# Loading a hybrid encoder's two short row groups as half rows over all partitions, casting the first block by channel halves, and splitting the last scaling

## The chip, the cores and the metric

One core of a Trainium2 chip. The metric is the device time in microseconds (us); lower is better. Three runs of the kernel before gave 919.87, 920.51 and 922.76 us, so its median is 920.51 us. The profile is of one more execution, which took 922.18 us.

## The reference, cut to what matters

One layer of an encoder over 2048 prompt frames and 32 sample frames of 1024 channels, all in float32:

```python
hn   = rmsnorm(h, g_mix)                       # h * rsqrt(mean(h*h) + 1e-6) * g_mix
proj = hn @ w_in                               # 1024 -> 3072: hA, bA, cA, zA, vB, zB, 512 each
yA   = bA * conv3(cA * hA) * silu(zA)          # short causal convolution
yB   = (pool(vB) @ pool_w) * pool_scale * silu(zB)
h    = h + concat(yA, yB) @ w_out
gate = sigmoid(rmsnorm(h, g_ple) @ w_ple_gate)
h    = h + (p @ w_ple) * gate
y    = rmsnorm(h, g_final)
```

It returns y for prompt and sample, and the last rows of the two mixers' inputs as states. The change touches the first line for the first frames, and the last line for the last frames.

## The kernel before, in words

The 2080 frames go through three stages on one core: the input projection with both mixers (frames as columns), the output projection, and the gate with the final norm (frames as rows). A float32 product is made of three TensorE products of "hi" and "lo" parts: hi is the operand rounded to the format fp32r, lo is the operand minus hi, and hi·hi, hi·lo and lo·hi are added in PSUM.

**Blocks.** In the first stage the frames are cut in five blocks of 416 (NB, line 25). A block is three tiles of 128 rows and one short group of 32 rows. The rows must be normalized while they are rows (one rstd for each) and then turned, so that channels lie on the partitions: eight TensorE transposes for a tile of 128 rows, four for each half of the channels.

**The start** (lines 382 to 724), on which most of the change bears. SyncE (SP) issues the loads in this order: the norm's weights gm_row (L383); the x rows of block 0's tiles 0, 1 and 2, of 512 KB each, and then the short group, as rows 384 to 415 of block 0 and of block 1 on 64 partitions, one load of 128 KB for each block (all L412, called at lines 630 and 631); the weights of the first three products, raw_firstzb, raw_firstv and raw_firstc, 512 KB each in rows of 512 bytes (L529); six small loads into rows (L772 to L777); raw_pw (L790); and then the three tiles of block 1 (L412 again). For each tile:

- ScalarE (ACT) squares the rows and sums them (L93); GpSimd (POOL) makes the mean (L72) and the power -1/2 (L76);
- VectorE (DVE) multiplies by rstd and by the norm's weights, which lie in two PSUM banks pg[0] and pg[1], one half of the channels each (L641, two instructions a tile);
- TensorE transposes (L433 for tiles, L650 for the short group) into a PSUM bank for each half;
- first_hi (L663) casts a turned half to fp32r, on ACT but for the last one, which is on DVE; first_lo (L667) subtracts, on DVE.

fill (L393) sends TensorE transposes of the identity that nobody reads: seven before the first tile, and two, three and two behind tiles 0, 1 and 2 (line 673). The hi parts of the first weights are cast on ACT (L694, L712), their lo parts on DVE (L703, L716). first_products (L601) then makes three products side by side, zb, v and c, in passes: all hi·hi first, then weight hi by frame lo, then weight lo by frame hi, 8 matmuls of 416 columns for each product and pass (L621). Between them block 1 is prepared step by step (second_block, L728); its short group is the other half of the short tile.

**Order.** A scheduler orders each engine's instructions when the program is built. in_turn (L633) takes an instruction out of its hands: it goes behind all that the program has issued on that engine up to there. In before the first zb matmul alone is not held (L623). PSUM has six banks in one pool (bank) and two in another (tbank); a bank is given to a new tile when the last reader of the old one is done.

**The end** (last_pair, L1587). The last two row tiles are scaled by their rstd in normed (L1633): DVE does 640 of the 1024 columns (L1637), which SP stores (L1638), ACT does 384 (L1639), which are stored through the queue of POOL for the first of the two tiles and of ACT for the last one (L1640).

Of the kernel before, what the change touches and what calls it, by code (L numbers as in the profile page):

```python
# [9 lines left out]
F32 = mybir.dt.float32  # L10
# [24 lines left out]
def trunk(ctx, tc, x_p, x_s, c_conv, c_pool, p_p, p_s, g_mix, w_in, conv_w, conv_b, pool_w,  # L35
# [308 lines left out]
    with ExitStack() as s1:  # L344
# [53 lines left out]

        hn = {}
# [201 lines left out]
        def first_products(ws):  # L601
# [6 lines left out]
            for a, b in ((0, 0), (0, 1), (1, 0)):  # L608
                if b:
                    next(second)  # L610
                    next(second)
                for kind, w in ws.items():
# [7 lines left out]
                    for k in range(KC):  # L620
                        ins = nc.tensor.matmul(out[kind][:, :NB], w[k // KH][:, k % KH, a], x[k // KH][:, k % KH, b],  # L621
                                               start=a + b + k == 0, stop=a == 1 and k == KC - 1, skip_group_check=True)
                        if a + b + k or kind != "zb":  # L623
                            in_turn(ins)
# [5 lines left out]
        ahead0 = [x_load(f"0_{c}", [x_rows(0, c)]) for c in range(3)]  # L630
        short0 = x_load("0_3", [x_rows(0, 3), x_rows(1, 3)])
# [4 lines left out]
        def first_normal(x):  # L636

            xt, m, r = x
            for half in range(2):
# [3 lines left out]
        def first_turn(c, x):  # L643

            xt, m, _ = x
            if c < 3:
                return [turn(x, half, f"pt0_{c}_{half}", bank) for half in range(2)]
            t = short_bank
            for k in range(KC):
                tc.keep_in_program_order(nc.tensor.transpose(t[:, k * m:k * m + m], xt[:m, k * P:(k + 1) * P], ident[:m, :m]))  # L650
            t = t.rearrange("p (k t) -> p k t", k=KC)
            return t[:, :KH], t[:, KH:]
# [3 lines left out]
        def place0(c, half):  # L656
            n = P if c < 3 else DEC
            piece = B0[("11", "21")[half]][:, :, :, c * P:c * P + n]
            return piece[:, :, 0], piece[:, :, 1], turned_x[c][half][:, :, :n]
# [9 lines left out]
        def first_tile(c):  # L669
            first_normal(first_x[c])  # L670
            turned_x[c] = first_turn(c, first_x[c])
            if c < 3:
                fill((2, 3, 2)[c], short_bank)


        for c in range(3):
            first_x.append(x_stat(ahead0[c], True))
        first_tile(0)
        first_hi(0, 0)
        first_x.append(x_stat(short0, True))  # L680
        short0 = first_x[3]
        first_tile(1)
        first_hi(0, 1)
        first_lo(0, 0)
        for half in range(2):
            first_hi(1, half)
        first_tile(2)
        first_hi(2, 0)
        first_tile(3)
        first_hi(2, 1, nc.vector.tensor_copy)  # L690
        raw = raw_weight("zb", 0, "firstzb")
        first_zb = [wtile(f"w_firstzb_{half}") for half in range(2)]
        for half, t in enumerate(first_zb):
            in_turn(nc.scalar.copy(t[:, :, 0], raw[:, half * KH:half * KH + KH]))  # L694
        for half in range(2):
# [1102 lines left out]
```

## Time and profile before

| what | before |
|---|---|
| median of three runs | 920.51 us (919.87 to 922.76) |
| the profiled execution, whole | 922.18 us |
| its span in the trace | 920.4 us |
| TensorE matmuls (PE), busy in the span | 907.0 us, 99% |
| VectorE (DVE), busy | 723.2 us, 79% |
| ScalarE (ACT), busy | 482.7 us, 52% |
| GpSimd (POOL), busy | 159.3 us, 17% |
| granted TensorE clock | 0.998 |

How to read the profile: times in the trace are us from the start of the span. A row of the timeline gives the start, the time from there to the end of the last one of the group, the engine, the source line, the operation, what it writes and reads with the shapes, how many of them there are, and in brackets how long the engine was idle before it and what released it. PE is TensorE's matmul, PEld its weight load; a transpose appears as a weight load of the rows and a matmul with the identity. SPq, ACTq and POOLq rows are DMA issues. L12 is line 12 of the kernel.

### The profile page before, as it was taken

What the parts mean: (1) busy time and instruction counts of PE and PEld (TensorE: products, weight loads), DVE (VectorE), ACT (ScalarE), POOL (GpSimd) and SP (SyncE); (2) the same over time, 40 slices, a digit from 0 to 9 for tenths busy, and PEclk for the clock granted to TensorE, in tenths of its full rate; (3) what the DMA queues carried; (4) which work ended last, traced back from release to release, by engine and by line L of the source; (5) the groups of instructions that cost most, each with busy time, mean ns of one, the idle gap of its engine ahead of it and who ended that gap; (6) DMA issues with size and microseconds to landing.
All of it is one profiled execution on the core that took longest, in us unless ns stands there. A gap on an engine that the chain in (4) does not pass through costs nothing.

```text
span 920.4 us, 13201 instructions
## 1 busy us (share of the span) xinstructions
PE 907.0 (99%) x4529; PEld 824.7 (90%) x4529; DVE 723.2 (79%) x1236; ACT 482.7 (52%) x894; POOL 159.3 (17%) x307
## 2 busy tenths in 40 slices
PE   8999999999999999999999999999999999999996
PEld 6999999999999999999999988888878878888885
DVE  6996898999576989795777579666558658889885
ACT  6744565654345555453444365444436855555554
POOL 2111222121000342310000111111113301111113
PEclk9999999999999999999999999999999999999999
DMA  8357687898945789738885468865767974576554
GB/s 247 100 141 220 170 245 230 244 282 285 416 137 172 235 231 221 231 115 303 245 243 178 146 234 278 266 218 183 237 228 230 357 262 140 206 242 231 190 201 176
DMA packets 138447, 205.12 MB, mean 223 GB/s; under 512 B 13116, under 2 KB 101724, under 8 KB 137101
## 3 DMA queue, kind: packets, MB, share of 16 engines
q1 hardware_dynamic: 117773, 139.41, 47.9%
q0 software_dynamic: 17872, 59.45, 19.6%
q10 hardware_dynamic: 2736, 5.44, 1.6%
q8 instruction: 35, 0.57, 0.3%
q14 instruction: 31, 0.25, 0.1%
HBM read 136.60 MB, written 67.64 MB: 222 GB/s over the span
## 4 chain that ended last, share of the span: by engine, by line
PE 78%; DVE 6%; DMA 3%; issue 1%; ACT 1%; POOL 0%; POOLq 0%; DVEq 0%
PE x_o L175 9%; PE x_g L175 9%; PE x_zab L593 5%; PE z_g L175 5%; PE x_zbv L593 5%; PE e L107 4%; PE z_o L175 4%; PE x_ch L593 4%; PE z_zab L593 3%; PE z_zbv L593 2%; PE z_ch L593 2%; PE y_g L175 2%; PE y_o L175 2%; PE za L593 2%; PE b L593 2%; PE h L593 1%
## 5 line engine op out<-in xcount | busy, mean ns | idle before, releaser
L80 ACT CAST y_S<-y_fS 128x512 fp32r<-128x512 f32 x32 | 19.5, 622 | 36.8 <-PE x_o L175 19.0
L175 PE MATMUL x_g<-wg_b,g_S 128*128 128x512 f32 x128 | 35.7, 390 | 0.0
L175 PE MATMUL x_o<-wo_b,y_S 128*128 128x512 f32 x128 | 35.7, 391 | 0.0
L593 PE MATMUL x_zab<-B,w_zab_S 128*128 128x416 f32 x168 | 34.2, 352 | 0.2 <-ACT V L989 0.2
L593 PE MATMUL z_zab<-B,w_zab_S 128*128 128x416 f32 x168 | 34.3, 352 | 0.0
L593 PE MATMUL x_zbv<-B,w_zbv_S 128*128 128x416 f32 x168 | 34.2, 352 | 0.0
L593 PE MATMUL z_ch<-B,w_ch_S 128*128 128x416 f32 x168 | 34.1, 352 | 0.0
L593 PE MATMUL x_ch<-B,w_ch_S 128*128 128x416 f32 x168 | 34.0, 351 | 0.0
L593 PE MATMUL z_zbv<-B,w_zbv_S 128*128 128x416 f32 x168 | 34.0, 351 | 0.0
L107 PE MATMUL e<-wq,pps 128*128 128x512 f32 x144 | 33.1, 390 | 0.0
L593 PEld LDWEIGHTS x_zab<-B,w_zab_S 128*128 128x128 f32 x168 | 31.3, 188 | 0.8 <-ACT V L989 0.5
L107 PEld LDWEIGHTS e<-wq,pps 128*128 128x128 f32 x144 | 27.0, 188 | 5.6
L593 PEld LDWEIGHTS x_ch<-B,w_ch_S 128*128 128x128 f32 x168 | 31.4, 188 | 0.3
L593 PEld LDWEIGHTS z_zbv<-B,w_zbv_S 128*128 128x128 f32 x168 | 31.4, 188 | 0.3
L593 PEld LDWEIGHTS z_ch<-B,w_ch_S 128*128 128x128 f32 x168 | 31.4, 188 | 0.3
L593 PEld LDWEIGHTS z_zab<-B,w_zab_S 128*128 128x128 f32 x168 | 31.4, 188 | 0.3
L593 PEld LDWEIGHTS x_zbv<-B,w_zbv_S 128*128 128x128 f32 x168 | 31.3, 188 | 0.4
L1343 DVE TENSOR_TENSOR c_o<-x_o,x 128x512 f32<-128x512 f32 x14 | 9.7, 691 | 26.4 <-PE x_o L175 26.4
L1566 DVE SCALAR_TENSOR_TENSOR h<-h,rstd_f,g_bc 128x1024 f32<-128x1024 f32 (+1 forms) x15 | 19.3, 1284 | 14.0 <-POOL rstd_f L76 14.0
L72 POOL TENSOR_SCALAR ms_f<-ssq_f 128x1 f32<-128x1 f32 (+1 forms) x15 | 6.6, 441 | 128.7 <-ACT junk L93 128.5
L175 PEld LDWEIGHTS x_o<-wo_b,y_S 128*128 128x128 f32 x128 | 24.0, 188 | 5.2 <-DVE c_o L1343 0.3
L175 PEld LDWEIGHTS x_g<-wg_b,g_S 128*128 128x128 f32 x128 | 24.0, 188 | 5.0
(591 smaller groups left out, 2688.5 us busy)
## 6 DMA issues: line engine op xcount, KB each, us to landing
y<-y_d SPq DMA_DIRECT2D x16, 512.0 KB, 6.7
x<-in_x_prompt_dram SPq DMA_DIRECT2D x16, 512.0 KB, 4.3
h_d<-x SPq DMA_DIRECT2D x16, 512.0 KB, 3.8
h<-h_d SPq DMA_DIRECT2D x16, 512.0 KB, 3.7
xt<-in_x_prompt_dram SPq DMA_DIRECT2D x15, 512.0 KB, 7.2
e<-e_d SPq DMA_DIRECT2D x15, 512.0 KB, 6.3
out_dram<-h POOLq DMA_DIRECT2D x14, 512.0 KB, 3.0
p_dT<-T POOLq DMA_DIRECT2D x12, 512.0 KB, 6.0
```

The lines of the kernel that those rows point to most:

```text
L72: nc.gpsimd.tensor_scalar(ms[:n], ssq[:n], scalar1=1.0 / D, scalar2=EPS, op0=ALU.mult, op1=ALU.add)
L80: ins = nc.scalar.copy(hi, src)
L107: nc.tensor.matmul(ps, pps[:, a, k], wp[k][b][:, cs], start=k + q == 0, stop=k == 1 and q == 2)
L175: nc.tensor.matmul(ps[:n], lhs[:, k, a, :n], w[b][:, k], start=start and k + q == 0, stop=k == KH - 1 and q == 2, skip_group_check=True)
L593: nc.tensor.matmul(ps[:, :NB], lhs[:, k, x], b[:, k, y], start=start and k + q == 0, stop=stop and k == KH - 1 and q == 2, skip_group_chec ...
L1343: add = lambda o, a, b: nc.vector.tensor_tensor(o, a, b, op=ALU.add)
L1566: nc.vector.scalar_tensor_tensor(h[:n], h[:n], rf[:n], g_bc[:n], op0=ALU.mult, op1=ALU.mult)
```

## The change

The short group now lies as half rows on all 128 partitions: partitions 0 to 63 hold channels 0 to 511 of the 64 short rows, partitions 64 to 127 hold channels 512 to 1023 of the same rows. It is loaded in two loads, one for each half of the channels, both ahead of tile 2. Its sums of squares are therefore half sums, and a matmul with a matrix called pair adds partitions p and p + 64. Its mean is made on DVE out of PSUM. Normalizing takes two instructions of 64 partitions, as before, and the transposes come in two groups of four.

The order of the start is rewritten: the short group's square comes before tile 2's; pg[0] is copied to SBUF early on ACT; tile 2's second half is turned into a bank of the other PSUM pool; the hi casts come by halves of the channels, with the first weights' casts in between; the lo parts come by halves too. The fills behind tiles 0, 1 and 2 are gone; the seven ahead of tile 0 stay. All matmuls of the first products are held in program order, behind the last transposes of the short group, and the transpose of rows (pv) moves behind the first pass.

At the end, for the last tile only, DVE's 640 columns are scaled in two instructions of 320, each with a store of its own on SP.

```diff
+        HP = P // 2
+        pair = one.tile([P, P], F32, name="pair")
+        for h in range(2):
+            nc.vector.tensor_tensor(pair[:, h * HP:h * HP + HP], ident[:, :HP], ident[:, HP:], op=ALU.add)
...
                 if b:
+                    vectors()
                     next(second)
...
-                        if a + b + k or kind != "zb":
-                            in_turn(ins)
+                        in_turn(ins)
...
-        ahead0 = [x_load(f"0_{c}", [x_rows(0, c)]) for c in range(3)]
-        short0 = x_load("0_3", [x_rows(0, 3), x_rows(1, 3)])
+        ahead0 = [x_load(f"0_{c}", [x_rows(0, c)]) for c in range(2)]
+
+        short_x = ring4(xin, "xt_short")
+        for h in range(2):
+            nc.sync.dma_start(short_x[h * HP:h * HP + HP, :NH],
+                              x_p[:2 * NB, h * NH:h * NH + NH].rearrange("(b n) d -> b n d", b=2)[:, 3 * P:])
+        ahead0.append(x_load("0_2", [x_rows(0, 2)]))
...
+            gets = (bank, tbank if c == 2 else bank)
+            return [turn(x, half, f"pt0_{c}_{half}", gets[half], True) for half in range(2)]
+
+        def short_turn(half, t, pin=lambda ins: None):
+
+            hs = slice(half * HP, half * HP + HP)
+            for k in range(KH):
+                pin(nc.tensor.transpose(t[:, k * HP:k * HP + HP], short_x[hs, k * P:k * P + P], ident[hs, hs]))
+            return t.rearrange("p (k b t) -> p k b t", k=KH, b=2)
+
+        def short_sums():
+            ssq = sm.tile([P, 1], F32, tag="ssq", name="ssq_short")
+            in_turn(nc.scalar.activation(junk[:, :NH], short_x[:, :NH], AF.Square, accum_out=ssq))
+            return ssq
+
+        def short_root(ssq):
+            in_turn(nc.tensor.matmul(short_bank[:, :1], pair, ssq, start=True, stop=True))
+            ms, r = (sm.tile([P, 1], F32, tag=t, name=f"{t}_short") for t in ("ms", "rstd"))
+            in_turn(nc.vector.tensor_scalar(ms, short_bank[:, :1], scalar1=1.0 / D, scalar2=EPS, op0=ALU.mult, op1=ALU.add))
+            nc.gpsimd.tensor_tensor(r, ms, nhalf, op=ALU.pow)
+            return r
+
+        def short_half(half, r):
+            hs = slice(half * HP, half * HP + HP)
+            h = short_x[hs, :NH]
+            in_turn(nc.vector.scalar_tensor_tensor(h, h, r[hs], pg[half][hs], op0=ALU.mult, op1=ALU.mult))
+            n = KH * HP
+            turned_x[3, half] = short_turn(half, short_bank[:, half * n:half * n + n], in_turn)[:, :, 0]
...
-            if c < 3:
-                fill((2, 3, 2)[c], short_bank)
...
+        def zb_hi(half, copy=nc.scalar.copy):
+            in_turn(copy(first_zb[half][:, :, 0], raw[:, half * KH:half * KH + KH]))
...
+        for c in range(2):
+            first_x.append(x_stat(ahead0[c], True))
+        short_ssq = short_sums()
+        g_copy = lambda half: nc.scalar.copy(g_bc[:, half * NH:half * NH + NH], pg[half])
+        first_tile(0)
+        in_turn(g_copy(0))
+        first_x.append(x_stat(ahead0[2], True))
+        first_normal(first_x[1], halves=(1, 0))
+        short_r = short_root(short_ssq)
+        turned_x[1] = first_turn(1, first_x[1])
+        first_hi(0, 0)
+        first_hi(1, 0)
+        short_half(0, short_r)
+        first_normal(first_x[2], (0,))
+        first_lo(0, 0)
+        first_normal(first_x[2], (1,))
+        turned_x[2] = first_turn(2, first_x[2])
+        zb_hi(0)
+        first_hi(0, 1)
+        first_hi(3, 0)
+        first_hi(2, 0)
+        short_half(1, short_r)
+        first_hi(1, 1)
+        first_hi(2, 1, nc.vector.tensor_copy)
+        zb_hi(1)
+        first_hi(3, 1)
         for half in range(2):
+            for c in range(4):
                 if c + half:
                     first_lo(c, half)
...
-                fixed(nc.vector.tensor_scalar(o[:, :cut], o[:, :cut], scalar1=rf, scalar2=None, op0=ALU.mult))
-                nc.sync.dma_start(y[:, :cut], o[:, :cut])
+                for cs in (slice(0, cut // 2), slice(cut // 2, cut)) if b else (slice(0, cut),):
+                    fixed(nc.vector.tensor_scalar(o[:, cs], o[:, cs], scalar1=rf, scalar2=None, op0=ALU.mult))
+                    nc.sync.dma_start(y[:, cs], o[:, cs])
```

More of the change, by code (lines that the diff above doesn't have):

```diff
@@ L634, in in_turn, with first_normal @@
             tc.keep_in_program_order(ins)
-        def first_normal(x):
+        def first_normal(x, halves=(0, 1)):
             xt, m, r = x
-            for half in range(2):
+            for half in halves:
                 h = xt[:m, half * NH:half * NH + NH]
@@ L722, in trunk @@
         first_w.extend(other_first(kind) for kind in ("v", "c"))
-        for half in range(2):
-            nc.scalar.copy(g_bc[:, half * NH:half * NH + NH], pg[half])
+        g_copy(1)
         B0["12"] = piece_of(seventh("B0_12"), 0)
@@ L736, in second_block @@
                 yield
[L737 removed]
+            xs.append(((short_x, DEC, None), None))
             whole = []
```

48 lines of the change are left out of this document (12 added, 36 removed).

## The prediction

> **What bounds the kernel now.** First the page: the shares of the engines, then the chain that ended last.
>
> ```profile
> span 920.4 us, 13201 instructions
> PE 907.0 (99%) x4529; PEld 824.7 (90%) x4529; DVE 723.2 (79%) x1236; ACT 482.7 (52%) x894; POOL 159.3 (17%) x307
> PE 78%; DVE 6%; DMA 3%; issue 1%; ACT 1%; POOL 0%; POOLq 0%; DVEq 0%
> ```
>
> TensorE is busy in 907.0 of 920.4 us, and the change leaves its products as they are. So only the 13.4 us without it count, and they lie mostly ahead of the first product and behind the last one. A microsecond at the start reaches the end as it is, unless a later wait takes it up. Next the list of waits, PE's rows:
>
> ```profile
> PE gm L388 <- DVE V L826: 2.3, 1, 2.3
> PE pt_g L433 <- DVE 11_1_1_1643 L83: 1.1, 1, 1.1
> PE zb L621 <- DVE B L667: 0.8, 1, 0.8
> PE pt L433 <- DVE xt L641: 0.7, 1, 0.7
> ```
>
> Two of the four are the start that the change rewrites; the one for pt_g lies in the next block group. The timeline of the start shows what the first product waits for:
>
> ```profile
> 1.14 2.48 SPq L412 DMA_DIRECT2D xt<-in_x_prompt_dram  x5
> 4.39 1.06 ACT L93 ACTIVATE junk<-xt 128x1024 bf16<-128x1024 f32 x1 [2.17 <-DMA xt<-in_x_prompt_dram]
> 5.90 1.06 ACT L93 ACTIVATE junk<-xt 128x1024 bf16<-128x1024 f32 x1 [0.35 <-DMA xt<-in_x_prompt_dram]
> ...
> 6.49 2.91 DVE L641 SCALAR_TENSOR_TENSOR xt<-xt,rstd_x,gm 128x512 f32<-128x512 f32 x4 [4.30 <-POOL rstd_x L76]
> ...
> 9.68 1.06 ACT L93 ACTIVATE junk<-xt 128x1024 bf16<-128x1024 f32 x1 [2.64 <-DMA xt<-in_x_prompt_dram]
> ...
> 10.92 0.19 POOL L72 TENSOR_SCALAR ms_x<-ssq_x 128x1 f32<-128x1 f32 x1 [2.96 <-ACT junk L93]
> ...
> 11.19 0.55 POOL L76 TENSOR_TENSOR rstd_x<-ms_x,nhalf 128x1 f32<-128x1 f32 x1
> ...
> 11.34 0.69 DVE L667 TENSOR_TENSOR B<-pt,B 128x512 fp32r<-128x512 f32 x1 [1.94 <-ACT B L663]
> 11.94 2.73 DVE L641 SCALAR_TENSOR_TENSOR xt<-xt,rstd_x,gm 128x512 f32<-128x512 f32 x4
> ...
> 12.26 2.00 ACT L663 CAST B<-pt 128x512 fp32r<-128x512 f32 x4
> ...
> 14.15 1.15 ACT L694 CAST w_firstzb<-raw_firstzb 128x512 fp32r<-128x512 f32 x2
> 14.26 0.79 PEld L650 LDWEIGHTS pt<-ident,xt 64*128 64x128 f32 x8 [0.17 <-issue]
> ...
> 15.23 0.43 ACT L663 CAST B<-pt 128x128 fp32r<-128x128 f32 x2
> ...
> 15.99 1.43 PEld L621 LDWEIGHTS zb<-B,w_firstzb 128*128 128x128 f32 x8 [0.94 <-ACT B L663]
> 16.02 1.75 PE L621 MATMUL zb<-B,w_firstzb 128*128 128x416 f32 x8 [0.83 <-DVE B L667]
> ```
>
> The chain starts with tile 2. ACT waits 2.64 us for it, until 9.68; its rstd comes at 11.74, its normalizing at 11.94, then transposes and casts, and zb at 15.99. So **zb starts 6.31 us after tile 2 has landed**. Whatever delays tile 2 delays everything.
>
> **The change, part by part: behind tile 2.** Normalizing starts 2.26 us after the landing (11.94 less 9.68); the same square, mean, power and DVE step stand there after the change. Behind it the held order on DVE is tile 2's first half, first_lo(0,0), tile 2's second half, the short group's second half. Four L641 take 2.73 us and one takes 0.74 by the row below, so their pitch is 0.66; first_lo has 0.60 (11.34 to 11.94). That is 2.26 + 0.66 + 0.60 + 0.66 + 0.74 = 4.92 us after the landing. PE follows 0.06 later (12.68 to 12.74 for tile 2 now) with four transposes, half of the eight in 0.79 us, so 0.40.
>
> ```profile
> 11.94 0.74 DVE L641 SCALAR_TENSOR_TENSOR xt<-xt,rstd_x,gm 128x512 f32<-128x512 f32 x1
> 12.74 0.42 PEld L433 LDWEIGHTS pt<-ident,xt 128*128 128x128 f32 x4 [0.97 <-DVE xt L641]
> 9.40 1.72 PEld L433 LDWEIGHTS pt<-ident,xt 128*128 128x128 f32 x8
> 5.93 1.35 PEld L393 LDWEIGHTS pt<-ident 128*128 128x128 f32 x7 [1.50 <-POOL ms_x L72]
> 11.11 0.66 PEld L393 LDWEIGHTS pt<-ident 128*128 128x128 f32 x3
> ```
>
> zb is now held behind these transposes, so it starts **5.38 us after tile 2's landing** instead of 6.31: 0.93 gained. The casts by halves can't bring more, because the held zb waits for the second half's last transposes anyhow; they only spare it a further wait. Its second four matmuls come 0.7 us later (half of 1.43) and need the short group's last cast, which fits: that cast takes 0.2 to 0.3 us on ACT (two in 0.43). The zb wait for first_lo goes too, since a bank is free from first_lo(0,0) on. The weights' casts move on ACT between others and stay off the chain.
>
> **Ahead of tile 2.** The two short loads, 256 KB, now stand ahead of tile 2 in SP's queue. The squares of tiles 0 and 1 start 1.51 us apart, so 16 engines move 512 KB in 1.51 us, 32 KB each. What the short rows cost lies between two ends. Spread evenly they are 16 KB an engine, 0.75 us at most: tile 2 lands at 10.43, zb starts at 15.81, 0.18 earlier than now. But the source of each short load is 2 blocks of 32 rows, with the 2 outermost; every other x load has its 128 or 32 rows outermost. If a transfer is dealt out along its outermost dimension, two engines carry all 256 KB, 128 KB each: 4 times 1.51, or 6.0 us. That tile 2 has to wait for the fullest engine shows in the packet counts:
>
> ```profile
> DMA packets 106, 0.37 MB, mean 369 GB/s; under 512 B 16, under 2 KB 16, under 8 KB 106
> DMA packets 350, 0.20 MB, mean 195 GB/s; under 512 B 4, under 2 KB 345, under 8 KB 350
> ```
>
> These are the windows 6 to 7 and 9 to 10 us. 90 packets of 4 KB (x rows) move in the first, five in the last; those five hold up the tile until 9.68 while the others already carry weights. On two engines tile 2 comes after tile 1's 5.90 by 6.0 and its own 1.5: 13.4. At the rate of 6 to 7 us (369 GB/s; 512 KB in 1.51 us are 347) it is 7.1 behind 5.90, 13.0; if the two engines run faster while they carry nothing but this, some 12.2 (my estimate, from an eighth more than that rate). I take 12.8. Then zb starts at 18.18: **2.2 us later**, from 1.5 (12.2) to 2.8 (13.4). The nearest row by bytes is the even end (the short loads of before), but it differs in just the dimension that decides; I go by the shape.
>
> The Trainium skill (DMA: Bandwidth & Descriptors, section "Why a DMA increments its semaphore by 16 and not by 1") says that the number of engines is the largest one up to 16 that divides the outermost sizes of both sides. Here these are 2 and 64, so it would be two; no run so far shows a load of this shape, and by the even end the sum would be 2.4 us lower.
>
> The waits that this adds: ACT's short square waits for its rows, at 12.8 less 1.4, or 11.4; behind it on ACT stand the copy of pg[0], tile 2's square and all casts, which need tile 2 anyhow. On PE the pair matmul waits for the sums, and tile 1's eight transposes stand behind it, so they move from 9.40 to some 13; their casts are due at 14.3, so this is hidden. On DVE the short mean waits, and the short first half: 11.4 + 1.06 + 0.55 + 0.74 and a mean of 0.2 (as L72) and a matmul, which I bound by nothing and by one transpose's 0.215 twice over, make 14.4, ahead of tile 2's 15.06. With one engine emptied late, the weights behind come later too:
>
> ```profile
> SPq L412 <- DMA raw_firstc<-in_w_in_dram: 1.3, 1, 1.3
> 16.05 1.36 SPq L412 DMA_DIRECT2D xt<-in_x_prompt_dram  x3
> 19.53 1.06 ACT L93 ACTIVATE junk<-xt 128x1024 bf16<-128x1024 f32 x1 [0.30 <-DMA xt<-in_x_prompt_dram]
> 25.11 0.98 PEld L433 LDWEIGHTS pt<-ident,xt 128*128 128x128 f32 x8
> ```
>
> SP issues block 1's rows only when firstc is there (16.05). Those rows shift by about what zb shifts, so PE meets them as now; if the two engines are also the late ones of now, by 2 us more, and that is in the upper end.
>
> **The fills.** Seven transposes take 1.35 us, and tile 1's eight still 1.72, 0.215 each; at 12.74 four take 0.42, 0.105 each. So TensorE was slow through the fills up to 11.77 at least and twice as fast from 12.74, though the granted clock reads 1.00 throughout. It had been nearly without a gap since 5.93. With the change PE stands idle from some 9 to 13 us and has gaps after that. If it needs its 6 us of dense work anew from zb on, half of them are lost, 3.0 us, and the last eight transposes cost another 0.6; if the transposes from 13 us on are enough, nothing. I take 1.2, nearer the low end, since they fill some four fifths of the time up to zb.
>
> The Trainium skill (TensorE: Matmul & The Clock Gate, Part 4) says that transposes don't count as busy work for the clock. By it the missing fills would cost nothing; the rows speak against it, since transposes and four one-row matmuls are all that PE had done by 12.74.
>
> **The small rest.** Two pair additions on DVE at the start lie in its 4.30 us idle before 6.49; POOL loses one mean and SP issues as many x loads as before. pv moves by one pass, with its matmul. The end:
>
> ```profile
> 915.61 0.55 DVE L1637 TENSOR_SCALAR hg<-hg,rstd_l 128x640 f32<-128x640 f32 x1 [0.83 <-POOL rstd_l L1630]
> 916.19 0.34 SPq L1638 DMA_DIRECT2D out_dram<-hg  x1
> 916.26 0.38 ACTq L1640 DMA_DIRECT2D out_dram<-hg  x1
> ```
>
> Half the columns take between 0.28 and 0.42, say 0.35, so the first store leaves at 915.99, 0.20 earlier, and the second, behind the first's issue of 0.34, at 916.33, 0.14 later. ACT's store doesn't move. Between -0.2 and +0.14 I take -0.1.
>
> **Sum:** +2.2 + 1.2 - 0.1 = +3.3 us. The profiled execution took 922.18 us, 1.8 over its span and 1.7 over the median of 920.51; set against that median, 920.51 + 3.3 = **923.8 us**.
>
> **The rivals.** *The short loads are spread evenly and the clock comes in time* (the side that isn't slower): -0.18 at the start and -0.1 at the end, or 920.2, down to 919.4 if tile 2 keeps its 9.68. It decides by one number: tile 2's square before 10.6 us means no loss. For it speaks that all short loads in the trace do well; against it the shape. *The loads are spread, but without the fills the clock comes late:* tile 1's transposes end at 11.1 and PE rests until 12.7; 0.6 for cold transposes and some 1.7 of the 3.0 give -0.3 + 2.3, or 922.5. *The change doesn't do what it says:* the casts by halves gain nothing because zb is held; this is already in the sum. A version that gains 3 us has no place in the profile: the whole wait ahead of zb is 16 us, of which the x rows' landing takes 9.68.
>
> **How the numbers follow.** Two engines: 0.72, from 921.8 (1.5 late, no clock loss, -0.2) to 926.2, near the top of both terms. Even and in time: 0.18. Even with a late clock: 0.10. The range 920.0 to 926.2 leaves out half of the second case and the upper corner of the first. 0.3%, 2.8 us, is about what a measurement of this kernel can tell from no change. Over +2.8 lies some two thirds of the first case and little of the third: slower 0.49. Within: 0.46. Faster by more needs a shift that I don't see, such as another order by the scheduler further on: 0.05.
>
> **What would show it.** Tile 2's square (L93, the fourth) near 12.8 us and x packets on two engines until then: the loads. zb 5.4 to 6.0 us behind it: the held order. zb's eight weight loads in 1.43 us or up to twice that: the clock. The last store issued at 916.3 plus the shift. If tile 2's square stands before 10.6 us, the main step was wrong; if the whole shift is gone by 200 us, a later wait has taken it up.

## The result, and the profile after

| what | before | after |
|---|---|---|
| median | 920.37 us (919.75 to 922.76, 6 runs) | 929.89 us (929.47 to 930.91, 6 runs) |
| ratio, 95% interval | 1 | 1.0102 [1.0089, 1.0115] |
| the profiled execution, its span | 922.18 us, 920.4 us | 929.51 us, 927.7 us |
| granted clock over the span | 0.998 | 0.991 |

The change makes the kernel **slower by 9.5 us, 1.0%**. The forecast was 923.8 us with a range up to 926.2: the sign was right, the size was not. Four executions of the experiments below, one each of e3, e4, e5 and e11, took 998 to 1129 us; the ratios leave them out, and as e11's was the profiled one (997.91), its trace isn't read. The timeline of the start, after:

```profile
6.15 1.06 ACT L93 ACTIVATE junk<-xt 128x1024 bf16<-128x1024 f32 x1 [0.17 <-DMA xt<-in_x_prompt_dram]
...
13.17 0.63 ACT L667 ACTIVATE junk<-xt_short 128x512 bf16<-128x512 f32 x1 [5.87 <-DMA xt_short<-in_x_prompt_dram]
...
13.80 0.56 ACT L714 COPY g_bc<-gm 128x512 f32<-128x512 f32 x1
...
14.31 1.06 ACT L93 ACTIVATE junk<-xt 128x1024 bf16<-128x1024 f32 x1
14.40 0.75 DVE L652 SCALAR_TENSOR_TENSOR xt<-xt,rstd_x,gm 128x512 f32<-128x512 f32 x1 [5.40 <-ACT g_bc L714]
...
15.82 0.55 POOL L76 TENSOR_TENSOR rstd_x<-ms_x,nhalf 128x1 f32<-128x1 f32 x1
16.33 0.55 POOL L674 TENSOR_TENSOR rstd_short<-ms_short,nhalf 128x1 f32<-128x1 f32 x1
...
16.91 0.74 DVE L680 SCALAR_TENSOR_TENSOR xt_short<-xt_short,rstd_short,gm 64x512 f32<-64x512 f32 x1 [1.70 <-POOL rstd_short L674]
...
17.58 0.73 DVE L652 SCALAR_TENSOR_TENSOR xt<-xt,rstd_x,gm 128x512 f32<-128x512 f32 x1
```

ACT waits 5.87 us for the short rows, until 13.17. Tile 2's square (14.31) no longer waits for its own rows, as it did in the kernel before, but stands behind the short square and a copy on ACT. Below it two more rows in brackets matter: DVE waited 5.40 us for that copy before it could do tile 1's first half, and the short rows' rstd stands on POOL behind tile 2's (16.33 behind 15.82), so DVE waits for it until 16.91 and tile 2's first half comes after that. The windows 11 to 15 us show who carried the short rows (the last three columns are the granted clock, the mean busy share of the 16 DMA engines, and GB/s):

```profile
11.00:12.00 1.00, 0.00 (x0) 0.00 (x0) 0.00 (x0) 0.00 (x0) 0.00 (x0) 1.00 0.67 135
12.00:13.00 1.00, 0.00 (x0) 0.00 (x0) 0.00 (x0) 0.00 (x0) 0.00 (x0) 0.86 0.19 56
13.00:14.00 1.00, 0.06 (x1) 0.06 (x1) 0.00 (x0) 0.83 (x3) 0.00 (x0) 0.50 0.14 44
14.00:15.00 1.00, 0.53 (x2) 0.44 (x2) 0.60 (x1) 1.00 (x2) 0.00 (x0) 0.50 0.22 54
```

A share of 0.14 is 2.2 engines of 16, roughly: the share counts up to 1.22 where all are at work (before, 9 to 10 us). Everybody else waits, all four compute engines are at rest for whole microseconds, and the clock granted to TensorE falls to 0.50. What that costs stands in the weight loads' rows:

```profile
21.28 2.58 PEld L628 LDWEIGHTS zb<-B,w_firstzb 128*128 128x128 f32 x8
23.88 2.65 PEld L628 LDWEIGHTS v<-B,w_firstv 128*128 128x128 f32 x8
26.53 1.51 PEld L628 LDWEIGHTS c<-B,w_firstc 128*128 128x128 f32 x8
```

zb starts at 21.28 in place of 15.99 and runs at about half speed, and so does v; c is at full speed. From there on the two traces run in step. A mark for that is the first matmul of pm, at 43.51 before and 50.97 after: 7.46 later, and the spans differ by 7.3. What comes later neither takes the loss up nor adds to it.

7.3 in the profiles is less than 9.5 in the medians. The profiled execution of before was itself 1.8 above its median; where it lost that is settled by the second profiles (last group of experiments).

### The profile page after: what moved, and what is told of

Read it like the earlier page. It is cut to its first block, busy times and chain, and to the rows that moved or that the text cites. A ratio compares the mean times of both kernels' runs of the same rounds, so it can differ in the third digit from the quotient of the medians.

```text
span 927.7 us, 13194 instructions
## 1 busy us (share of the span) xinstructions
PE 910.3 (98%) x4524; PEld 825.7 (89%) x4524; DVE 722.9 (78%) x1240; ACT 482.3 (52%) x894; POOL 157.6 (17%) x306
## 4 chain that ended last, share of the span: by engine, by line
PE 87%; DMA 5%; DVE 4%; ACT 2%; issue 1%; SPq 0%; POOL 0%; POOLq 0%; DVEq 0%; ACTq 0%
PE x_o L175 9%; PE x_g L175 9%; PE x_zab L599 6%; PE x_zbv L599 6%; PE x_ch L599 5%; PE z_g L175 5%; PE e L107 4%; PE z_o L175 4%; PE z_zab L599 3%; PE z_zbv L599 3%; PE za L599 3%; PE z_ch L599 3%; PE b L599 3%; PE y_g L175 2%; PE y_o L175 2%; PE h L599 2%
```

## The experiments

Shown as ratio to the kernel before measured on the same chip, with the 95% interval. "Mark" is the start of the first pm matmul.

| run | median us | ratio | tile 2's square | zb | mark |
|---|---|---|---|---|---|
| before, profile 1 | 920.37 | 1 | 9.68 | 15.99 | 43.51 |
| after | 929.89 | 1.0102 [1.0089, 1.0115] | 14.31 | 21.28 | 50.97 |
| e1 after, four loads | 922.74 | 1.0020 [1.0011, 1.0029] | 8.94 | 15.68 | 44.14 |
| e2 before, one load of [2, 32, 1024] | 928.19 | 1.0076 [1.0058, 1.0094] | 7.40 | 19.49 | 48.50 |
| e3 e1 and fills | 924.35 | 1.0036 [1.0024, 1.0047] | 9.06 | 16.43 | 45.32 |
| e4 before, split end | 920.33 | 0.9991 [0.9980, 1.0001] | 9.42 | 15.73 | 43.26 |
| e5 after, one of two loads split | 926.32 | 1.0065 [1.0050, 1.0081] | 12.56 | 19.54 | 48.66 |
| e6 e1 and fills in other columns | 923.68 | 1.0040 [1.0026, 1.0054] | 9.07 | 16.44 | 45.33 |
| e7 after, order only | 926.51 | 1.0073 [1.0060, 1.0085] | 14.37 | 19.77 | 47.79 |
| e8 e6 and order | 923.80 | 1.0039 [1.0025, 1.0052] | 9.30 | 16.01 | 44.87 |
| e9 e1, fills with the others' order kept | 922.31 | 1.0017 [1.0006, 1.0028] | 9.13 | 15.72 | 44.07 |
| e10 e1, tile 2 ahead of the short half, fills | 922.21 | 1.0015 [1.0005, 1.0026] | 9.06 | 16.14 | 43.91 |
| e11 e1, fills ahead only | 921.09 | 1.0008 [1.0000, 1.0017] | | | |
| e12 e10, fills ahead only | 921.01 | 1.0009 [1.0001, 1.0018] | 8.84 | 14.61 | 42.42 |
| e13, e14 before again, one execution each | 921.00, 920.51 | | 8.05, 8.49 | 14.56, 14.80 | 42.07, 42.33 |
| e15 e12 again, one execution | 920.53 | | 8.84 | 14.61 | 42.35 |
| e16 after again, one execution | 928.27 | | 14.77 | 21.74 | 50.13 |

The sessions ran on different chips, so medians of different rows are best compared by their ratios. The execution of the kernel before that was taken beside e13 to e16 took 924.18 us.

### The loads: taken away, put in, halved

**e1** takes the shape away from the changed kernel:

```diff
-            nc.sync.dma_start(short_x[h * HP:h * HP + HP, :NH],
-                              x_p[:2 * NB, h * NH:h * NH + NH].rearrange("(b n) d -> b n d", b=2)[:, 3 * P:])
+            for b in range(2):
+                nc.sync.dma_start(short_x[h * HP + b * DEC:h * HP + b * DEC + DEC, :NH],
+                                  x_rows(b, 3)[:, h * NH:h * NH + NH])
```

> The kernel after, with the short rows' two loads made four: one for each block and half of the channels, 32 rows outermost in each, same bytes at the same place in SP's queue. Theory (the loads with 2 outermost run on two engines, and all behind them waits): the short square starts by 9 us instead of 13.17, tile 2's square near 10.5 instead of 14.31, zb between 15.5 and 17.5 instead of 21.28, and the time falls to 922.5 to 925.5, according to whether the clock comes in time. Rival (the loads land late for their place in the queue or their 2 KB rows, or the held order is what costs): the short square stays near 13, and the time at 929 to 930.

Its timeline:

```profile
7.74 0.63 ACT L668 ACTIVATE junk<-xt_short 128x512 bf16<-128x512 f32 x1
...
8.94 1.06 ACT L93 ACTIVATE junk<-xt 128x1024 bf16<-128x1024 f32 x1
...
15.68 2.52 PEld L628 LDWEIGHTS zb<-B,w_firstzb 128*128 128x128 f32 x8
```

The same bytes in the same rows of 2 KB, on their way 5.4 us shorter: ACT doesn't wait for the short rows at all (7.74, no bracket). By the ratios, 1.0102 and 1.0020, some 7.5 us of the 9.5 are gone.

**e2** puts the shape into the kernel before, where the short rows come last:

```diff
-        short0 = x_load("0_3", [x_rows(0, 3), x_rows(1, 3)])
+        short0 = ring4(xin, "xt_0_3"), 2 * DEC, "x0_3"
+        nc.sync.dma_start(short0[0][:2 * DEC], x_p[:2 * NB].rearrange("(b n) d -> b n d", b=2)[:, 3 * P:])
```

> The kernel before, with one thing changed: its two short loads of 32 rows each are one load of the same 64 rows on 64 partitions, whose source has the 2 blocks outermost. It still stands behind tile 2. Theory (two engines): tile 2's square stays at 9.7, the short square moves from 11.2 to 14 to 15, and as ACT's later casts stand behind it, zb moves from 16.0 to 18.5 to 20; time 923 to 927. Rival (the shape of the load does not matter): zb at 16.0 and 920 to 921.

Its timeline and, below, two of its windows:

```profile
7.40 1.06 ACT L93 ACTIVATE junk<-xt 128x1024 bf16<-128x1024 f32 x1 [0.40 <-DMA xt<-in_x_prompt_dram]
...
14.66 1.06 ACT L93 ACTIVATE junk<-xt 64x1024 bf16<-64x1024 f32 x1 [5.31 <-DMA xt<-in_x_prompt_dram]
...
19.49 2.58 PEld L621 LDWEIGHTS zb<-B,w_firstzb 128*128 128x128 f32 x8 [0.80 <-ACT B L664]
```

```profile
12.00:13.00 1.00, 0.67 (x7) 0.43 (x4) 0.00 (x0) 0.00 (x0) 0.00 (x0) 1.00 0.16 53
13.00:14.00 1.00, 0.00 (x0) 0.00 (x0) 0.00 (x0) 0.00 (x0) 0.00 (x0) 1.00 0.12 45
```

0.12 of 16 engines is 1.9. The 256 KB land 7.26 us behind tile 2 (14.66 less 7.40), so 128 KB an engine cost 7.3 us: nearly the same as in the changed kernel, 7.0 from the square of tile 1 at 6.15 to 13.17. So the price doesn't hang on the half rows (4 KB rows here, 2 KB there) or on the place in the queue. The median is 7.4 us over the 920.8 that the kernel before took beside it (7.0 by the ratio), more than the 923 to 927 us that I expected. zb at 19.49 is within its forecast, but its eight loads took 2.58 us in place of 1.43, and tile 2 had landed at 7.40 and not at 9.7.

**e5** is the dose: the first half as two loads of 32 rows, the second as it was.

```diff
+            if h:
                 nc.sync.dma_start(short_x[h * HP:h * HP + HP, :NH], ...)
+            else:
+                for b in range(2):
+                    nc.sync.dma_start(short_x[b * DEC:b * DEC + DEC, :NH], x_rows(b, 3)[:, :NH])
```

> The changed kernel with the short rows' first half loaded as two loads of 32 rows and the second half kept as one load with 2 outermost: half the bytes that went through two engines. Theory (a load with 2 outermost runs on two engines, and what lies behind it on those engines waits): the time follows the bytes an engine has to carry, 64 KB in place of 128 KB, so the short rows land about halfway between the 7.7 us or less of four loads and the 13.17 us of the changed kernel, 9.5 to 10.5 us, zb starts at 17.5 to 18.7 us (15.68 with four loads, 21.28 in the changed kernel), and the time is about 925 to 927 us. Rival (it is the count of slow loads that decides, each waiting for the other, or a fixed cost of such a load): then one slow load alone either costs nothing (923 us, as four loads) or as much as two (930 us).

Its timeline:

```profile
11.47 0.63 ACT L671 ACTIVATE junk<-xt_short 128x512 bf16<-128x512 f32 x1 [3.90 <-DMA xt_short<-in_x_prompt_dram]
...
12.56 1.06 ACT L93 ACTIVATE junk<-xt 128x1024 bf16<-128x1024 f32 x1
...
19.54 2.58 PEld L628 LDWEIGHTS zb<-B,w_firstzb 128*128 128x128 f32 x8
```

The time falls between the two, as forecast (926.32), but the rows land at 11.47, not at 9.5 to 10.5, and zb starts at 19.54, not at 17.5 to 18.7: half the bytes cost 5.05 us behind tile 1's square at 6.42, not half of 7. By bytes alone that isn't explained, and it stays open whether the rest is a fixed part or the weights that the same two engines carry meanwhile.

The Trainium skill (DMA: Bandwidth & Descriptors, section "Why a DMA increments its semaphore by 16 and not by 1") gives two engines for outermost sizes of 2 and 64; the shares 0.12 to 0.19, or 1.9 to 3.0 of 16, agree with it.

### The order

**e7** keeps the two loads and moves only what needn't wait for them; the short rstd is held ahead of tile 2's:

```diff
-        short_ssq = short_sums()
         ...
         in_turn(g_copy(0))
-        first_x.append(x_stat(ahead0[2], True))
         first_normal(first_x[1], halves=(1, 0))
-        short_r = short_root(short_ssq)
         turned_x[1] = first_turn(1, first_x[1])
         first_hi(0, 0)
+        first_lo(0, 0)
         first_hi(1, 0)
+        short_r = short_root(short_sums())
+        first_x.append(x_stat(ahead0[2], True))
         short_half(0, short_r)
-        first_normal(first_x[2], (0,))
-        first_lo(0, 0)
-        first_normal(first_x[2], (1,))
+        first_normal(first_x[2])
...
-            nc.gpsimd.tensor_tensor(r, ms, nhalf, op=ALU.pow)
+            in_turn(nc.gpsimd.tensor_tensor(r, ms, nhalf, op=ALU.pow))
```

> The changed kernel with its two loads kept, and only the order changed: the copy of gm's first half, the first two cast pieces of tiles 0 and 1 and the turning of tile 1 go ahead of the short rows' square on ScalarE and TensorE, the short rows' rstd is held ahead of tile 2's on GpSimd, and tile 0's rest goes ahead of the first half of the short rows on VectorE. Theory (the 6.97 us from tile 2's square to zb, against the 5.38 that I forecast, come from the copy of gm that tile 1 waits for and from rstd_short behind tile 2's rstd): tile 2's square still starts at about 14.3 us, short_half(0) at 15.2 to 15.6 in place of 16.91, and zb at 19.0 to 19.9 in place of 21.28; time about 927.5 to 928.5 us. Rival (the chain behind the square is set by its own lengths on VectorE and TensorE and not by those two waits): zb at 21.0 or later, time 929 to 930 us. If the denser TensorE work between 7 and 13 us moves the clock the other way, zb's eight weight loads show it (2.58 us in the changed kernel).

Its timeline:

```profile
13.20 0.63 ACT L667 ACTIVATE junk<-xt_short 128x512 bf16<-128x512 f32 x1 [1.84 <-DMA xt_short<-in_x_prompt_dram]
...
14.37 1.06 ACT L93 ACTIVATE junk<-xt 128x1024 bf16<-128x1024 f32 x1 [0.44 <-DMA xt<-in_x_prompt_dram]
...
15.21 0.74 DVE L680 SCALAR_TENSOR_TENSOR xt_short<-xt_short,rstd_short,gm 64x512 f32<-64x512 f32 x1 [0.66 <-POOL rstd_short L674]
...
17.26 1.57 PEld L439 LDWEIGHTS pt<-ident,xt 128*128 128x128 f32 x8 [0.75 <-DVE xt L652]
...
19.77 2.01 PEld L628 LDWEIGHTS zb<-B,w_firstzb 128*128 128x128 f32 x8
21.79 1.50 PEld L628 LDWEIGHTS v<-B,w_firstv 128*128 128x128 f32 x8
```

Rows and tile 2 land as before, but zb starts **5.40 us** behind tile 2's square in place of 6.97. That is the forecast's 5.38, but not quite by its terms: first_lo is no longer in the chain (0.6 less), and tile 2's eight transposes at half speed (1.57 us in e7) add about as much. The mark comes 3.2 us earlier than in the changed kernel, more than the 1.5 us of zb, since zb and v run faster (2.01 and 1.50 us in place of 2.58 and 2.65); so the time, 926.51, is under the 927.5 to 928.5 us that I expected. e7 also shows that tile 2 itself lands only at 14.37: where the copy and the short square don't hold it, its rows do.

### The clock

**e3** adds to e1 the fills of the kernel before (2, 3 and 2 transposes behind tiles 0, 1 and 2), in the short rows' bank. The last two write over the turned first half of the short rows, so y of those rows changes.

> The four-loads kernel with the fills put back: two, three and two transposes that nobody reads behind tiles 0, 1 and 2. Theory (without the fills TensorE's clock comes late): zb's and v's eight weight loads take 1.4 to 1.5 us each, as in the kernel before, and where the four-loads kernel without fills shows them slower the time falls below it by what they lose there, up to 2.3 us: 921 to 923. Rival (the clock went late only because PE stood idle behind the late short rows): zb is at full speed in both and the two times agree within 0.5 us.

**e6** does the same in columns that nobody reads:

```diff
             turned_x[c] = first_turn(c, first_x[c])
+            fill(2, short_bank[:, NH // 2:])
...
         turned_x[1] = first_turn(1, first_x[1])
+        fill(3, short_bank[:, NH // 2:])
...
         turned_x[2] = first_turn(2, first_x[2])
+        fill(2, short_bank[:, NH // 2:])
```

> The run with four loads, with the fills of 2, 3 and 2 transposes behind the three tiles as in the kernel before, but written to columns of the short rows' bank that nothing is waiting to read. Theory (what is left of the loss with four loads is the clock, 1.09 us on zb's eight weight loads at half speed): zb's first eight weight loads take 1.4 to 1.6 us in place of 2.52, zb starts within 0.3 us of 15.68, and the time falls by 0.8 to 1.2 us against four loads alone, to 921.5 to 922 us. Rival (fills bring nothing, since the clock follows something else than transposes, or since they delay the tiles' own transposes by as much as they save): zb's loads still take 2.5 us or zb starts at 16.5, and the time stays at 922.7 us or above.

By the ratios they cost 1.5 and 1.8 us over e1 in place of saving 1.1. e6's timeline says why:

```profile
15.15 0.58 ACT L716 COPY g_bc<-gm 128x512 f32<-128x512 f32 x1 [2.33 <-DVE xt_short L681]
15.63 1.26 ACT L695 CAST B<-pt 128x128 fp32r<-128x128 f32 x3
...
15.95 0.33 PEld L663 LDWEIGHTS pt<-ident,xt_short 64*128 64x128 f32 x4 [0.93 <-ACT B L695]
...
16.44 0.68 PEld L628 LDWEIGHTS zb<-B,w_firstzb 128*128 128x128 f32 x4 [0.17 <-ACT B L695]
```

The clock did come (0.68 for four loads). But the copy of gm's second half, which nothing holds in its place, had been scheduled ahead of the short rows' cast, because the fills shift the scheduler's reckoning; ACT waited 2.33 us in it, and the short rows' second turning for ACT. My first reading of e3, that the fills' columns were the trouble, fell with this.

**e8** puts e7's idea on e6 (four loads, fills, the short rstd first, tile 0's rest in the gap ahead of the short half).

> All three repairs together: four loads, the fills in columns of their own, and the short rows' rstd held ahead of tile 2's with tile 0's rest in the gap ahead of it. Theory (the change lost by its two-outermost loads, by the clock and by that order, and its other parts gain): zb starts at 14.8 to 15.3 us, its eight weight loads take 1.4 to 1.6 us, the offset to the kernel before behind the first three products is -0.6 to -1.2 us, and the time is 919.3 to 920.6 us: equal to the kernel before or up to 0.15% faster. Rival (the short rows as half rows cost more in the chain than they save, whatever the loads): zb at 15.7 or later and 921.5 us or more.

zb at 16.01 and 923.80 us: the rival's side, but with 1.29 us in the same misplaced copy, so it tells nothing of the order.

**e9** places seven fills so that no other engine's order changes (5 behind tile 1's turning, 1 and 1 among the later ones).

> The run with four loads and seven fills in places where they change no other engine's order (five behind tile 1's turning, one ahead of each half of tile 2's second and first turning), in columns of their own. In the two runs with the fills of 2, 3 and 2, ScalarE had its copy of gm's second half ahead of the short rows' first cast piece, and waited 2.33 to 2.45 us there; here it stands where it stands with four loads alone. Theory (the clock is the rest of the loss with four loads): zb starts within 0.2 us of 15.68, its eight weight loads take 1.4 to 1.6 us in place of 2.52, the offset to the kernel before behind zb is -0.4 to 0.0 us in place of +0.77, and the ratio to the kernel before falls from 1.0020 to 1.000 to 1.001. Rival (fills do not hold the clock, or hold up the tiles' own transposes): zb's loads still at 2.5 us, or zb later than 16.0, and the ratio stays at 1.002.

```profile
14.91 1.24 ACT L695 CAST B<-pt 128x128 fp32r<-128x128 f32 x3 [1.76 <-PE pt L393]
...
15.72 0.68 PEld L628 LDWEIGHTS zb<-B,w_firstzb 128*128 128x128 f32 x4
...
17.41 0.68 PEld L628 LDWEIGHTS zb<-B,w_firstzb 128*128 128x128 f32 x4 [1.01 <-ACT B L695]
```

In e9's timeline the loads are fast and zb starts on time, but ACT's cast of the short rows waited 1.76 us for a fill (L393) in the same bank, though in other columns, and zb's second half 1.01 us for ACT. Half right: fills hold the clock, and here they cost as much as they save.

**e11** has fills of 2 and 3 only ahead of the short rows' first turning, all else in e1's order.

> Four loads, with fills of 2 behind tile 0's turning and 3 behind tile 1's, and none later; every other instruction of every engine stands where it stands with four loads alone. In the run before this one with fills among the later turnings, the fills share a PSUM bank with the short rows, and ScalarE's cast of the short rows' first half waited 1.76 us for them and TensorE 1.01 us for that. Here no fill stands between the first turning of the short rows and zb, so that wait cannot arise. Theory (the clock is the rest of the loss with four loads, and a fill pays if nothing has to wait for its bank): tile 1's turning takes 1.1 to 1.4 us, zb starts at 15.4 to 15.8 us, its eight loads take 1.4 to 1.9 us in one piece, the offset to the kernel before behind zb is -0.3 to +0.2 us (0.77 with four loads alone), the ratio 1.000 to 1.001. Rival (the sparse stretch from 12.3 to 15 us lets the clock fall again, whatever ran before): zb's loads at 2.3 us or more, offset 0.6 or above, ratio 1.0015 to 1.002.

921.09 us, ratio 1.0008: 1.1 us under e1 by the ratios, which is what e1 loses at half speed. The two intervals overlap, so this agrees with the theory and doesn't prove it.

### The end, and the repaired whole

**e4** is the kernel before with the split last scaling alone.

> The kernel before with only the end changed: the last tile's 640 columns on VectorE in two pieces with a store each. Theory: the first store leaves 0.2 us earlier and the second 0.1 to 0.2 later, so the end moves by -0.2 to +0.15 us: 920.2 to 920.6 where the kernel before has 920.4. Rival (two stores cost a further completion each): 0.5 us or more slower.

```profile
915.27 0.68 DVE L1638 TENSOR_SCALAR hg<-hg,rstd_l 128x320 f32<-128x320 f32 x2 [0.83 <-POOL rstd_l L1630]
915.68 0.81 SPq L1639 DMA_DIRECT2D out_dram<-hg  x2
```

From this scaling to the end of the span (919.9) are 4.63 us, against 4.79 in the kernel before (920.4 less 915.61) and 4.58 in the changed one: 0.16 to 0.21 gained, at the good end of the forecast's bounds and too little for a median to tell. The other profiles agree: 4.77 and 4.75 without the split (e13, e14), 4.61 with it (e16).

**e10** and **e12** turn the order round: tile 2's first half goes ahead of the short rows' first half, with e10's fills at 5, 1 and 1 and e12's at 2 and 3 ahead of it.

```diff
-        short_half(0, short_r)
         first_normal(first_x[2], (0,))
-        first_lo(0, 0)
+        turned_x[2] = [turn(first_x[2], 0, "pt0_2_0", bank, True)]
+        short_half(0, short_r)
         first_normal(first_x[2], (1,))
-        turned_x[2] = first_turn(2, first_x[2])
+        turned_x[2].append(turn(first_x[2], 1, "pt0_2_1", tbank, True))
...
+        first_hi(2, 0)
         first_hi(3, 0)
-        first_hi(2, 0)
         short_half(1, short_r)
         first_hi(1, 1)
+        first_lo(0, 0)
...
-        g_copy(1)
+        in_turn(g_copy(1))
```

> Four loads, fills that keep clear of the rest (five, one and one), the copy of gm's second half held at its place, and the order of the short rows turned round: tile 2's first half goes ahead of the short rows' first half on VectorE and TensorE, so that rstd_short behind tile 2's rstd on GpSimd holds nothing up; tile 0's rest stands behind the short rows' second half. Theory (the change's half rows and casts by halves gain once the loads, the clock and the order are repaired): zb starts at 14.6 to 15.1 us, its loads take 1.4 to 1.6 us with up to 0.6 us of waiting between its halves, the offset to the kernel before behind zb is -0.8 to -1.3 us and the ratio 0.9985 to 0.9995. Rival (what VectorE and ScalarE have to do between tile 2's square and zb sets the start, whatever the order): zb at 15.4 or later, offset above -0.5 us, ratio 0.9995 to 1.001.

> The order with tile 2's first half ahead of the short rows' first half, four loads, and the fills of 2 and 3 ahead of it alone. Theory (in the last run of this order five fills at half speed held tile 2's turning from 11.91 to 12.92 us and two later ones held the short rows' casts; without them the order gains): tile 2's first turning starts at 11.9 to 12.2 us, zb at 14.6 to 15.2 us, its loads take 1.4 to 1.9 us, with a wait of up to 0.5 us between its halves, the offset to the kernel before behind zb is -0.5 to -1.3 us and the ratio 0.9985 to 0.9997. Rival (the work between tile 2's square and zb sets the start at about 15.5 us in any order): zb at 15.4 or later, ratio 0.9997 to 1.001.

In e10 five fills at half speed stood in front of tile 2's turning (11.86 to 12.92, in its way since 11.91); zb at 16.14 and a ratio of 1.0015 are the rival's side. e12's timeline:

```profile
8.84 1.06 ACT L93 ACTIVATE junk<-xt 128x1024 bf16<-128x1024 f32 x1
9.33 0.45 PEld L393 LDWEIGHTS pt<-ident 128*128 128x128 f32 x2
...
9.76 0.31 PEld L672 LDWEIGHTS pt<-ssq_short,pair 128*128 128x128 f32 x2
...
14.61 1.43 PEld L628 LDWEIGHTS zb<-B,w_firstzb 128*128 128x128 f32 x8 [0.44 <-PE pt L663]
```

zb at 14.61, as the theory had it, and yet the ratio is 1.0009, the rival's. The second profiles of before resolve that.

### Second profiles

> The kernel before once more, unchanged, for a second profile of it. The first profiled execution took 922.18 us, 1.8 above the median. Theory (that execution was late somewhere behind the first products, where single executions differ by waits of about 1 us, and its front is typical): zb starts at 15.6 to 16.2 us again, its eight loads take 1.43 to 1.6 us, and the difference to the first profile arises behind 100 us. Rival (the front itself varies from one execution to the next, by the time at which the clock rises): zb starts at 15.2 us or earlier, or its loads take over 1.8 us.

> The kernel before a third time, for the spread: by the theory of the run above zb starts within 0.4 us of 15.99 us in all three profiles; by its rival the three differ by 0.8 us or more.

> The last run of the series (four loads, tile 2's first half ahead of the short rows' first half, fills of 2 and 3 ahead of it) once more, unchanged. Its profile had zb at 14.61 us, 1.38 ahead of the kernel before, while its median was 0.09% above. Theory (what it gains at zb is typical and is lost behind, or the kernel before is faster than its profile showed): zb starts at 14.4 to 15.0 us again. Rival (its profile caught an early rise of the clock, at about 9.7 us): tile 1's turning at 1.4 us or more in place of 0.86, and zb at 15.3 us or later.

> The changed kernel once more, unchanged, for a second profile. Theory (what holds its front is the two loads, which do not vary): the short rows' square starts at 12.8 to 13.6 us and zb at 20.9 to 21.7 us, its loads 2.3 to 2.6 us. Rival (the landing through two engines varies by more than 1 us): outside of these.

The timelines of e13, e14 and e16:

```profile
8.05 1.06 ACT L93 ACTIVATE junk<-xt 128x1024 bf16<-128x1024 f32 x1 [0.67 <-DMA xt<-in_x_prompt_dram]
...
14.56 1.43 PEld L621 LDWEIGHTS zb<-B,w_firstzb 128*128 128x128 f32 x8 [0.72 <-ACT B L663]
```

```profile
8.49 1.06 ACT L93 ACTIVATE junk<-xt 128x1024 bf16<-128x1024 f32 x1 [0.90 <-DMA xt<-in_x_prompt_dram]
...
14.80 1.43 PEld L621 LDWEIGHTS zb<-B,w_firstzb 128*128 128x128 f32 x8 [0.78 <-ACT B L663]
16.23 1.51 PEld L621 LDWEIGHTS v<-B,w_firstv 128*128 128x128 f32 x8
```

```profile
13.57 0.63 ACT L667 ACTIVATE junk<-xt_short 128x512 bf16<-128x512 f32 x1 [6.16 <-DMA xt_short<-in_x_prompt_dram]
...
14.77 1.06 ACT L93 ACTIVATE junk<-xt 128x1024 bf16<-128x1024 f32 x1
...
21.74 2.45 PEld L628 LDWEIGHTS zb<-B,w_firstzb 128*128 128x128 f32 x8
24.19 1.51 PEld L628 LDWEIGHTS v<-B,w_firstv 128*128 128x128 f32 x8
```

The rival of e13 holds, but not by the clock that it named: what varied is **the landing of tile 2**, 8.05, 8.49, 9.42 (e4) and 9.68, and zb follows it by 6.31 us in three of these four and by 6.51 in the fourth. The first profile, on which the prediction was built, had the latest landing of the four. Whether the landing varies from one execution to the next or from chip to chip isn't shown: e13 and e14, on one chip, differ by 0.44 us. The changed kernel's front is nearly as it was (zb 21.28 and 21.74, the second a little later than expected), but not its clock: in e16 v's loads are at full speed. e12's front is as it was (zb at 14.61 twice). So e12 has zb where e13 and e14 have it, and with a ratio of 1.0009 it isn't faster.

## Why the prediction was right in its direction and wrong in its size

e14 took 920.51 us, close to the median of before, so its trace is a better ground than the first. Against it the changed kernel's profile is 9.0 us longer and e16 is 7.8 longer:

| step | forecast us | measured us, from the profile after | from e16 |
|---|---|---|---|
| tile 2's square | +3.1 (9.68 to 12.8) | +5.8 (8.49 to 14.31) | +6.3 (8.49 to 14.77) |
| from there to zb | -0.93 (6.31 to 5.38) | +0.66 (6.31 to 6.97) | +0.66 (6.31 to 6.97) |
| the clock, zb and v | +1.2 | +2.3 (21.28 to 26.53 is 5.25; 14.80 to 17.73 in e14, 2.93) | +1.0 (21.74 to 25.70, 3.96) |
| behind it, to the end | -0.1 | +0.2 (the remainder of 9.0) | -0.2 (the remainder of 7.8) |

Two steps failed in both profiles: the time that tile 2 lands, mis-sized, and the chain behind it, which had the wrong sign.

**The two-outermost loads** were the right cause: e1 removes some 7.5 us by the ratios with nothing but that edit, e2 adds 7.0 by its ratio to a kernel without any other part of the change. The term was mis-sized in two ways. The price of 128 KB on one engine came out at 7.0 to 7.3 us where I took 6.0 at most from the pace of 16 engines; no run bore out the lower end of 12.2, by which two engines run faster while they carry nothing but this. So tile 2 came a microsecond above my upper end for it (14.37 in e7, where it waits for nothing but its rows, against 13.4). And its base was one execution's landing of 9.68, where e13 and e14 have 8.05 and 8.49. The range took in the cost's two ends but not the spread of the base, 1.6 us between four executions.

**The chain behind tile 2** failed where the prediction put "which need tile 2 anyhow" on what stands behind the short square on ACT. The copy of pg[0] stood there, and DVE's first half of tile 1, which reads the same bank, waited 5.40 us for it; the short mean came behind that on DVE, the short rstd behind tile 2's on POOL, and tile 2's first half behind both. The prediction had the short half ready at 14.4, ahead of tile 2; it started only at 16.91. e7 undoes this, takes first_lo(0,0) out of the chain as well, and has 5.40 us from tile 2's square to zb. That this is the forecast's 5.38 is partly luck, since the terms differ.

**The clock**: "transposes from 13 us on" were not enough: the last four before zb still took 0.50 us (20.67 in the changed kernel's timeline) where four fast ones take 0.32 or 0.33 (e6, e12). The loads of zb were at half speed in both profiles (2.58 and 2.45 us), those of v in the first alone, so the two lost 2.3 and 1.0 us, and the forecast's 1.2 lies between. The value was taken near the low end on the ground that four fifths of the time would be filled; from 13 to 21 us TensorE was busy for 5.71 of 8, or 0.71, and the granted clock stayed at 0.50 throughout. The busy share alone doesn't decide: in e6 TensorE was busy for 0.30 to 0.66 of each microsecond from 12 to 16, and zb's loads were fast (0.68 us for four). What brings the clock up stays open.

**The end** came out as forecast. **The casts by halves** were never tried alone. In e12 the chain is 5.77, 0.5 less than before's, but tile 2's square stands behind the short square and the copy on ACT (8.84, without a wait), and that takes the gain back. No version was measurably faster than the kernel before; with all repairs (e12) the ratio is 1.0009, its interval just above 1.

**The chances**: the case that came, two engines, had 0.72; the forecast of "slower by over 0.3%" got 0.49 because the size was too small.

## What to carry to other kernels

Look at the outermost dimension of each new load's two sides before anything else: 256 KB in loads with 2 outermost took 7.0 to 7.3 us here, and on a chain that begins with the landing of rows all of it went to the end. When an instruction is moved ahead in a held order, list for each engine what is now behind the waiting one, including readers of the same PSUM bank and the powers queued on POOL; here undoing both, with one step taken out of the chain, was worth 1.6 us. Before a sum is set against one profile, ask how much its first landing varies: here 1.6 us, half of the whole forecast.

## What the runs showed of the hardware that was not expected

- 128 KB on each of two DMA engines took 7.0 to 7.3 us, 64 KB 5.05 us; the even loads moved 32 KB an engine in 1.51.
- After a rest of TensorE of 3.1 us (9.57 to about 12.7, worked out from the 0.86 of that window) the changed kernel's granted clock read 0.50. It fell in e1 too, where TensorE was busy 0.46 to 0.74 of each microsecond from 12 to 15: the short rows' four transposes took 0.32 us at 12.34 and 0.50 at 15.06. In e6 it didn't fall, at 0.30 to 0.66 from 12 to 16.
- The clock's rise isn't set by TensorE's work alone. With the same rows on TensorE up to tile 1's turning, loads went to full speed between 9.33 and 9.76 us in e12, between 10.29 and 11.36 in e6, and only between 13.12 and 13.73 in e8. The Trainium skill (TensorE: Matmul & The Clock Gate, Part 1) speaks of a window of some 3.4 us that runs freely and doesn't begin with the kernel; the latest of these rises came 3.4 to 4.4 us behind the earliest (13.12 less 9.76, 13.73 less 9.33), about one such window, which fits but doesn't show it. Part 4 of that page of the Trainium skill, by which transposes don't count, doesn't fit: in e12 nothing but transposes and four one-row matmuls had gone before the rise.
- Through all the slow transposes at the start the granted clock read 1.00 (before, 9 to 12 us), and in e16 it read 1.00 from 8 to 24 us, with zb's eight loads at 2.45 us; at that place the weight loads' own durations are the better witness.
